# Linear ReLU attention on one core: loads in pairs of octets up to the end, and one order of work for all octets

## The chip, the cores and the metric

The kernel runs on one core of a Trainium2 chip. The metric is the device time of one execution in microseconds (us), as a median of several runs. A profile of one execution stands beside it; its times are counted from the first instruction of the program.

## The reference

Batch 8, 12 heads, sequence 512, head dimension 64, all in fp32. There are 96 heads in all (batch times heads), and each is independent.

```python
Q_feat = np.maximum(0, Q)
K_feat = np.maximum(0, K)
KV = np.einsum('bhkd,bhkv->bhdv', K_feat, V)
K_sum = np.sum(K_feat, axis=2)
numerator = np.einsum('bhqd,bhdv->bhqv', Q_feat, KV)
denominator = np.einsum('bhqd,bhd->bhq', Q_feat, K_sum)
return (numerator / (denominator[:, :, :, None] + 1e-10)).astype(np.float32)
```

Q, K and V are 12 MiB each in HBM, and so is the output.

## The kernel before

The 96 heads are cut into 12 **octets** of eight heads (`NO = 12`). An octet's K, V, Q and output are 1 MiB each in HBM. K and V of an octet come as two **groups** of four heads; octet `o` has the groups `2*o` and `2*o+1`. An octet's rows are spread over the 128 partitions so that each partition reads one contiguous piece.

**Loads.** K, V and Q are cast from fp32 to bf16 on the way, and these DMAs are issued by GpSimd (POOL). Octet 0 is a special case: its K and V are fetched in fp32 by SP and ACT at the start, and its Q by POOL. For octets 1 to 11 there is a ring of `RING = 6` octets in SBUF: `k_all`, `v_all` and `q_all`. Octet `o` lives in slot `(o - 1) % RING`. At the start octets 1 to 6 are fetched as three pairs (`FIRST`), with K, V and Q of a pair as one transfer each. Afterwards `store(o)`, which issues the store of octet `o` on POOL, is followed at once by `load_octet(o + RING)`, which refills the slot of octet `o`. For octets 7 and 8 K, V and Q are one transfer each. From octet 9 on (`PAIRS = NO - 3`) the two groups of K and V are transfers of their own, in the order K, V, K, V, Q. POOL's instructions run in order, so a load that waits holds back the stores and loads after it.

**Compute.** For a group, `prep` makes a masked, rectified copy of K and one masked copy of V on DVE (L195, L197). `prep_v` makes the other copy of V on ACT (L202) or DVE (L204). `kvs(o)` multiplies both groups on PE into `ps_kv` (L209) and evicts the result to `kvd` on ACT (`evac_kv`, L219). `qt(o)` transposes Q on PE (L230) and rectifies it on ACT (L238). `denom(o)` makes the denominators on PE and their reciprocals on DVE (L269 to L281). `out_t(o)` makes the transposed numerators on PE (L260) and copies them to `ot_sb` on ACT (L262). `backs(o)` transposes them back on PE (L287), multiplies them by the reciprocals into an output tile `o_sb` on DVE (L293) and calls `store(o)`. Each engine runs its instructions in the order of the program, which is written by hand (`manual_schedule`). The output tiles come from a pool `outp` of `DELAY + 2 = 7` buffers. The PSUM buffers of `out_t` and of the back transposition are shared: two with the tag `ps_out`.

**Order of a round.** In a steady round `o` the order is: `kvs(o)`, `prep` and `prep_v` of the first group of octet `o+1`, `backs(o-1)`, `denom(o)`, `out_t(o)`, `prep` and `prep_v` of the second group of octet `o+1`, `qt(o+1)`. So an octet's output is finished in the round after its own. From `SAME = NO - 4 = 8` on the order changes: `kvs(o+1)` comes after the second `prep` of the same round, and `backs(o)` stands at the round's end. The last two octets are written out by hand, with the groups of octet 11 multiplied and evicted one at a time, part of the evictions and one rectification on DVE, and the last store in two halves. `idle` issues matmuls whose results are not used.

Of the kernel before, what the change touches and what calls it, by code (L numbers as in the profile page):

```python
# [10 lines left out]
def kernel(  # L11
# [7 lines left out]
    nc = tc.nc  # L19
    B, H, S, D = Q.shape  # L20
    assert D == 64
    P = 128
    D1 = D + 1
# [4 lines left out]
    RQ = S * 8 // P  # L28
    NHG = 4
    U = RQ // 2  # L30
    NG = NH // NHG
    NO = NG // 2
# [3 lines left out]
    fp32 = mybir.dt.float32  # L36
    bf16 = mybir.dt.bfloat16
    Act = mybir.ActivationFunctionType
# [23 lines left out]
    NK = 2  # L62
# [26 lines left out]

    q_sb, k_sb, v_sb = {}, {}, {}  # L90

    PAIRS = NO - 3
    RING = DELAY + 1
    FIRST = (2, 2, 2)
    k_all = consts.tile([P, 2 * RING, R, D], bf16, name="k_all")
    v_all = consts.tile([P, 2 * RING, R, D], bf16, name="v_all")
    q_all = consts.tile([P, RING + 1, U, 2 * D], bf16, name="q_all")
# [6 lines left out]

    def load_kv(X, tile_, first, n):
        to = 2 * ((first // 2 - 1) % RING) + first % 2
        if n == 1:
            nc.gpsimd.dma_start(out=tile_[:, to].rearrange("p r d -> p (r d)"), in_=X[first], single_packet=True)  # L108
            return
        nc.gpsimd.dma_start(out=tile_[:, to:to + n].rearrange("p n r d -> p n (r d)"),  # L110
                            in_=X[first:first + n].rearrange("n p f -> p n f"), single_packet=True)

# [13 lines left out]
    load_q(0)  # L126
    make_identity(nc, ident)

    def load_octet(o, n=1):
        m = 1 if o >= PAIRS else 2 * n  # L130
        for g in range(2 * o, 2 * (o + n), m):
            load_kv(Kr, k_all, g, m)
            load_kv(Vr, v_all, g, m)
        load_q(o, n)

    o = 1
    for n in FIRST:
        load_octet(o, n)
        o += n
    assert o == RING + 1  # L140

    def zero_masks():
        for h in range(NHG):
# [48 lines left out]
    def prep(g):  # L192
        kf[g] = kfp.tile([P, R, 2, D], bf16, name="kf")
        for s in range(2):
            nc.vector.tensor_scalar(kf[g][:, :, s, :], k_sb[g], scalar1=0.0,  # L195
                                    scalar2=mask[:, 0, s:s + 1], op0=Alu.max, op1=Alu.mult)
        nc.vector.tensor_scalar(vo[g % NB][:, :, 0, 2:D + 2], v_sb[g], scalar1=mask[:, 1, 0:1],  # L197
                                scalar2=None, op0=Alu.mult)

    def prep_v(g, eng):  # L200
        if eng is nc.scalar:
            nc.scalar.activation(vo[g % NB][:, :, 1, 2:D + 2], v_sb[g], Act.Copy, scale=mask[:, 1, 1:2])  # L202
        else:
            nc.vector.tensor_scalar(vo[g % NB][:, :, 1, 2:D + 2], v_sb[g], scalar1=mask[:, 1, 1:2],  # L204
                                    scalar2=None, op0=Alu.mult)

    def mm_kv(g):
        for r in range(R):
            nc.tensor.matmul(  # L209
                ps_kv[:, g % 2, 0:2 * (D + 2)].rearrange("p (t d) -> p t d", t=2),  # L210
                kf[g][:, r, :, :].rearrange("p s d -> p (s d)"), vo[g % NB][:, r, :, 1:D4 - 1],
                start=(r == 0), stop=(r == R - 1), skip_group_check=True)


    def evac_kv(o, gs, share=False):
        for s in range(2):
            for c in range(2):
                copy = nc.vector.tensor_copy if share and c == 1 else nc.scalar.copy
                copy(  # L219
                    kvd[o % NK][64 * c:64 * c + 64, 4 * gs.start + s:4 * gs.stop:2,  # L220
                               c * D1:c * D1 + D1].rearrange(
                        "p (g t) d -> p g t d", t=2),
                    ps_kv[64 * s:64 * s + 64, gs, 0:2 * (D + 2)].rearrange(
                        "p g (t d) -> p g t d", t=2)[:, :, :, c:c + D1])


    def transp(o, i):
        ps = pqt.tile([P, U // 2, P], bf16, name="ps_qt")
        for u in range(U // 2):
            nc.tensor.transpose(ps[:, u, :], q_sb[o][:, i * (U // 2) + u, :], ident)  # L230
        return ps

    def relu_q(o, i, ps, eng=None):
        to = qt_sb[o % NZ][:, i * (U // 2):(i + 1) * (U // 2)]
        if eng is nc.vector:
            nc.vector.tensor_scalar(to, ps, scalar1=0.0, scalar2=None, op0=Alu.max)
        else:
            nc.scalar.activation(to, ps, Act.Relu)  # L238

    def qt(o):  # L240
        for i in range(2):
            relu_q(o, i, transp(o, i))


    def idle(n, o):
        for i in range(n):
# [2 lines left out]

    def out_t(o, halves=range(2)):
        if halves[0] == 0:
            ot[o] = otp.tile([P, U, 8, 16], fp32, name="ot_sb")
        q = qt_sb[o % NZ].rearrange("p u (h c) -> p u h c", h=8)
        for j in halves:
            ps = pou.tile([P, 4, U, 16], fp32, name="ps_ot", tag="ps_out")
            for i in range(4):
                h = 4 * j + i
                nc.tensor.matmul(ps[:, i], kvd[o % NK][:, h, 1:2 * D + 1], q[:, :, h, :],  # L260
                                 start=True, stop=True, skip_group_check=True)
            nc.scalar.copy(ot[o][:, :, 4 * j:4 * j + 4], ps.rearrange("p h u c -> p u h c"))  # L262
# [3 lines left out]
    def denom(o):  # L266
        ps = ps_den[:, 0].rearrange("p (u h c) -> p u h c", u=U, h=8)
        for u in range(U):
            nc.tensor.matmul(ps[:, u], qt_sb[o % NZ][:, u, :], kvd[o % NK][:, :, 0:2 * D1:2 * D1 - 1],  # L269
                             start=True, stop=True, skip_group_check=True)  # L270
        own = rcp.tile([P, U, 8, 2], fp32, name="own")
        nc.vector.scalar_tensor_tensor(
            own.rearrange("p u h c -> p u (h c)"), ps.rearrange("p u h c -> p u (h c)"), 1e-10,
            mask_h.rearrange("p h c -> p (h c)").unsqueeze(1).to_broadcast([P, U, 16]),
            op0=Alu.add, op1=Alu.mult)
        den = rcp.tile([P, RQ], fp32, name="den")
        nc.vector.tensor_reduce(out=den.rearrange("p (u c) -> p u c", c=2),  # L277
                                in_=own.rearrange("p u h c -> p u c h"), op=Alu.add,
                                axis=mybir.AxisListType.X)
        rec[o] = rcp.tile([P, RQ], fp32, name="rec")  # L280
        nc.vector.reciprocal(rec[o], den)  # L281
# [9 lines left out]
    def norm(o, j, ps, o_sb):  # L291
        rs = slice(16 * j, 16 * j + 16)
        nc.vector.tensor_tensor(o_sb[:, rs], ps,  # L293
                                rec[o][:, rs].unsqueeze(2).to_broadcast([P, 16, D]), op=Alu.mult)
# [3 lines left out]

    def store(o, o_sb):
        Ov = Or[o].rearrange("p (r d) -> p r d", d=D)  # L300
        if o == NO - 1:
            for j in range(2):
                rs = slice(RQ // 2 * j, RQ // 2 * (j + 1))
                nc.sync.dma_start(out=Ov[:, rs], in_=o_sb[:, rs])
            return
        if o >= NO - 2:
            nc.sync.dma_start(out=Ov, in_=o_sb)
            return
        nc.gpsimd.dma_start(out=Ov, in_=o_sb, single_packet=True)  # L309
        if 0 < o < NO - RING:  # L310
            load_octet(o + RING)

    def out_tile():
        return outp.tile([P, RQ, D], fp32, name="o_sb", tag="o_sb")

    both = slice(0, 2)
    zero8()
    nc.vector.tensor_copy(ident32, ident)
    nc.vector.tensor_reduce(out=mask8k, in_=ident32.rearrange("p (t s b) -> p s t b", t=4, s=2),
# [12 lines left out]
    def backs(o):  # L332
        o_sb = out_tile()
        for j in range(2):
            norm(o, j, back(o, j), o_sb)
        store(o, o_sb)

    def kvs(o):
        mm_kv(2 * o)
        mm_kv(2 * o + 1)  # L340
        evac_kv(o, both)

    SAME = NO - 4
    for o in range(NO - 2):
        if 0 < o <= SAME:
            kvs(o)
        prep(2 * o + 2)
        prep_v(2 * o + 2, nc.scalar)  # L350
        if 0 < o <= SAME:
            backs(o - 1)
        denom(o)
        out_t(o)
        prep(2 * o + 3)
        prep_v(2 * o + 3, nc.vector)
        if o >= SAME:
            kvs(o + 1)
        qt(o + 1)
        if o >= SAME:  # L360
            backs(o)

    o = NO - 2
    g = 2 * NO - 2
    prep(g)
    prep_v(g, nc.vector)
    denom(o)
    out_t(o)
    mm_kv(g)
    evac_kv(o + 1, slice(0, 1))  # L370
    prep(g + 1)
    prep_v(g + 1, nc.vector)

    o_sb = out_tile()
    norm(o, 0, back(o, 0), o_sb)
    ps = back(o, 1)
    mm_kv(g + 1)
    evac_kv(o + 1, slice(1, 2), share=True)
    for i in range(2):
        relu_q(o + 1, i, transp(o + 1, i), nc.vector if i == 1 else None)  # L380
    norm(o, 1, ps, o_sb)
    store(o, o_sb)
    idle(5, o + 1)
    out_t(o + 1, (0,))
    denom(o + 1)
    out_t(o + 1, (1,))
    idle(6, o + 1)
    backs(o + 1)
# [1 line left out]
_INS = ['Q', 'K', 'V']  # L390
_OUTS = [((8, 12, 512, 64), 'float32')]
# [25 lines left out]
```

## Time and profile before

| | |
|---|---|
| time, median of 3 runs | 126.11 us (126.09 to 126.37) |
| profiled execution, its own time | 126.86 us |
| span of that execution, first to last instruction | 125.1 us |
| mean granted TensorE clock | 0.931 |
| busy: PE, DVE, ACT, POOL | 86.3, 83.2, 80.6, 26.5 us |
| read from HBM, written to HBM | 37.75 MB, 12.58 MB |
| DMAs issued on POOL: loads, stores | 31, 10 |
| last store, its two halves issued on SP | 117.78 and 118.91 us |

Busy times are those of the engines themselves; what a sequencer does (waits, DMA issues of SP) is not counted. PE is TensorE, DVE VectorE, ACT ScalarE, SP SyncE. A line number such as L293 is a line of the kernel before. A DMA's landing is the time from its issue until its data is there.

### The profile page before, as it was taken

What the parts mean: (1) busy time and instruction counts of PE and PEld (TensorE: products, weight loads), DVE (VectorE), ACT (ScalarE), POOL (GpSimd) and SP (SyncE); (2) the same over time, 40 slices, a digit from 0 to 9 for tenths busy, and PEclk for the clock granted to TensorE, in tenths of its full rate; (3) what the DMA queues carried; (4) which work ended last, traced back from release to release, by engine and by line L of the source; (5) the groups of instructions that cost most, each with busy time, mean ns of one, the idle gap of its engine ahead of it and who ended that gap; (6) DMA issues with size and microseconds to landing.
All of it is one profiled execution on the core that took longest, in us unless ns stands there. A gap on an engine that the chain in (4) does not pass through costs nothing.

```text
span 125.1 us, 2615 instructions
## 1 busy us (share of the span) xinstructions
PE 86.3 (69%) x1067; PEld 77.6 (62%) x1067; DVE 83.2 (67%) x192; ACT 80.6 (64%) x112; POOL 26.5 (21%) x47
## 2 busy tenths in 40 slices
PE   0005884089898998959989897799596496888500
PEld 0005563089787897839978786698494494876400
DVE  2719716920997979797297984967909819977700
ACT  0009966544989989896598988658669466646000
POOL 6942020000100901203311122144333321000000
PEclk9999999558999999995999999859999999999995
DMA  4999999999999999999999999999999999999991
GB/s 84 389 321 206 212 210 217 214 210 210 215 219 208 212 212 218 214 321 419 217 204 307 282 218 264 324 212 238 347 214 226 356 224 216 349 422 424 430 390 76
DMA packets 9836, 32.67 MB, mean 261 GB/s; under 512 B 736, under 2 KB 736, under 8 KB 8160
## 3 DMA queue, kind: packets, MB, share of 16 engines
q0 software_dynamic: 9104, 28.31, 94.5%
q1 hardware_dynamic: 576, 3.15, 6.6%
q10 hardware_dynamic: 144, 1.05, 2.2%
q8 instruction: 8, 0.13, 0.4%
q14 instruction: 4, 0.03, 0.1%
HBM read 37.75 MB, written 12.58 MB: 402 GB/s over the span
## 4 chain that ended last, share of the span: by engine, by line
DMA 44%; DVE 23%; PE 19%; POOL 4%; ACT 2%; issue 2%; DVEq 1%; POOLq 0%
DMA q_all<-in_Q_dram 28%; DMA v_all<-in_V_dram 16%; DVE o_sb L293 13%; PE ps_kv L209 8%; PE ps_bk L287 6%; PE ps_qt L230 3%; DVE kf L195 3%; ACT ot_sb L262 2%; DVE vo_all L197 2%; PE ps_ot L260 1%; DVE vo_all L204 1%; POOL k_all L110 1%; POOL v_all L110 1%; DVE den L277 1%; DVEq L412 1%
## 5 line engine op out<-in xcount | busy, mean ns | idle before, releaser
L293 DVE TENSOR_TENSOR o_sb<-ps_bk,rec 128x1024 f32<-128x1024 f32 x24 | 28.3, 1218 | 20.0 <-PE ps_bk L287 20.0
L209 PE MATMUL ps_kv<-vo_all,kf 128*128 128x132 bf16 x352 | 26.9, 238 | 4.9 <-DVE vo_all L204 4.4
L209 PEld LDWEIGHTS <-kf 128*128 128x128 bf16 x352 | 24.8, 106 | 6.2 <-issue 3.5
L230 PE MATMUL ps_qt<-ident,q_all 128*128 128x128 bf16 x192 | 15.5, 245 | 15.9 <-DMA q_all<-in_Q_dram 15.8
L262 ACT COPY ot_sb<-ps_ot 128x1024 f32<-128x1024 f32 x24 | 24.0, 1013 | 3.8 <-PE ps_ot L260 2.9
L219 ACT CAST kvd<-ps_kv 64x260 bf16<-64x260 f32 (+1 forms) x46 | 16.5, 359 | 15.1 <-PE ps_kv L209 13.9
L238 ACT ACTIVATE qt<-ps_qt 128x1024 bf16<-128x1024 bf16 x23 | 22.4, 1025 | 3.6 <-PE ps_qt L230 3.5
L230 PEld LDWEIGHTS <-q_all 128*128 128x128 bf16 x192 | 13.7, 111 | 16.9 <-DMA q_all<-in_Q_dram 16.7
L287 PE MATMUL ps_bk<-ident,ot_sb 128*128 128x128 f32 x192 | 23.0, 273 | 0.4 <-ACT ot_sb L262 0.4
L287 PEld LDWEIGHTS ps_bk<-ident,ot_sb 128*128 128x128 f32 x192 | 20.8, 142 | 0.7 <-ACT ot_sb L262 0.7
L195 DVE TENSOR_SCALAR kf<-k_all,mask 128x1024 bf16<-128x1024 bf16 x44 | 18.3, 458 | 1.4 <-DMA k_all<-in_K_dram 1.3
L260 PE MATMUL ps_ot<-qt,kvd 128*128 128x256 bf16 x96 | 13.9, 272 | 6.2 <-DVE o_sb L293 5.5
L260 PEld LDWEIGHTS <-kvd 128*128 128x128 bf16 x96 | 8.9, 97 | 8.8 <-issue 7.0
L309 POOL DMA_DIRECT2D out_dram<-o_sb x10 | 5.5, 551 | 39.8 <-DVE o_sb L293 31.0
L202 ACT ACTIVATE vo_all<-v_all,mask 128x1024 bf16<-128x1024 bf16 x10 | 11.5, 1154 | 1.3 <-DMA v_all<-in_V_dram 1.2
L197 DVE TENSOR_SCALAR vo_all<-v_all,mask 128x1024 bf16<-128x1024 bf16 x22 | 10.6, 483 | 2.1 <-DMA v_all<-in_V_dram 2.1
L269 PEld LDWEIGHTS <-qt 128*128 128x128 bf16 x192 | 6.7, 96 | 4.9 <-ACT qt L238 2.0
L269 PE MATMUL ps_den<-kvd,qt 128*128 128x16 bf16 x192 | 7.3, 179 | 3.0 <-ACT kvd L189 1.7
L178 ACT ACT_TABLE_LOAD x1 | 1.3, 1283 | 9.7 <-DMA v_first<-in_V_dram 9.7
L204 DVE TENSOR_SCALAR vo_all<-v_all,mask 128x1024 bf16<-128x1024 bf16 x12 | 5.8, 480 | 0.0
L110 POOL DMA_DIRECT2D v_all<-in_V_dram x5 | 4.0, 810 | 7.8 <-ACT ot_sb L262 4.4
L108 POOL DMA_DIRECT2D k_all<-in_K_dram x6 | 3.6, 604 | 8.4 <-DMA q_all<-in_Q_dram 4.9
(36 smaller groups left out, 56.7 us busy)
## 6 DMA issues: line engine op xcount, KB each, us to landing
out_dram<-o_sb POOLq DMA_DIRECT2D x10, 1024.0 KB, 15.2
q_all<-in_Q_dram POOLq DMA_DIRECT2D x6, 512.0 KB, 13.8
k_all<-in_K_dram POOLq DMA_DIRECT2D x3, 1024.0 KB, 26.9
v_all<-in_V_dram POOLq DMA_DIRECT2D x3, 1024.0 KB, 31.0
q_all<-in_Q_dram POOLq DMA_DIRECT2D x3, 1024.0 KB, 35.1
k_all<-in_K_dram POOLq DMA_DIRECT2D x6, 256.0 KB, 13.4
v_all<-in_V_dram POOLq DMA_DIRECT2D x6, 256.0 KB, 12.3
v_first<-in_V_dram ACTq DMA_DIRECT2D x1, 1024.0 KB, 8.9
```

The lines of the kernel that those rows point to most:

```text
L195: nc.vector.tensor_scalar(kf[g][:, :, s, :], k_sb[g], scalar1=0.0, scalar2=mask[:, 0, s:s + 1], op0=Alu.max, op1=Alu.mult)
L197: nc.vector.tensor_scalar(vo[g % NB][:, :, 0, 2:D + 2], v_sb[g], scalar1=mask[:, 1, 0:1], scalar2=None, op0=Alu.mult)
L202: nc.scalar.activation(vo[g % NB][:, :, 1, 2:D + 2], v_sb[g], Act.Copy, scale=mask[:, 1, 1:2])
L209: nc.tensor.matmul(ps_kv[:, g % 2, 0:2 * (D + 2)].rearrange("p (t d) -> p t d", t=2), kf[g][:, r, :, :].rearrange("p s d -> p (s d)"), vo[ ...
L219: copy(kvd[o % NK][64 * c:64 * c + 64, 4 * gs.start + s:4 * gs.stop:2, c * D1:c * D1 + D1].rearrange("p (g t) d -> p g t d", t=2), ps_kv[6 ...
L230: nc.tensor.transpose(ps[:, u, :], q_sb[o][:, i * (U // 2) + u, :], ident)
L238: nc.scalar.activation(to, ps, Act.Relu)
L260: nc.tensor.matmul(ps[:, i], kvd[o % NK][:, h, 1:2 * D + 1], q[:, :, h, :], start=True, stop=True, skip_group_check=True)
L262: nc.scalar.copy(ot[o][:, :, 4 * j:4 * j + 4], ps.rearrange("p h u c -> p u h c"))
L269: nc.tensor.matmul(ps[:, u], qt_sb[o % NZ][:, u, :], kvd[o % NK][:, :, 0:2 * D1:2 * D1 - 1], start=True, stop=True, skip_group_check=True)
L287: nc.tensor.transpose(ps[:, 2 * v:2 * v + 2].rearrange("p c d -> p (c d)"), ot[o][:, 8 * j + v].rearrange("p h c -> p (h c)"), ident32)
L293: nc.vector.tensor_tensor(o_sb[:, rs], ps, rec[o][:, rs].unsqueeze(2).to_broadcast([P, 16, D]), op=Alu.mult)
```

## The change

The change has four parts.

- The loads of octets 1 to 10 come as five pairs and octet 11 alone (`RUNS`). K, V and Q of a pair are one transfer each, and so are K, V and Q of octet 11. The first three pairs are issued at the start as before. Octets 7 and 8 are issued after store 1, octets 9 and 10 after store 3, octet 11 after store 4. Before, octets 7 to 11 were issued one at a time after stores 1 to 5.
- All rounds, to the last, have the steady order. The last round has no `prep` or `qt`, and runs `backs(10)` and, at its end, `backs(11)`.
- Both groups of an octet are always evicted together on ACT, and Q is always rectified on ACT.
- The last store is one transfer on SP.

```diff
-    PAIRS = NO - 3
     RING = DELAY + 1
-    FIRST = (2, 2, 2)
+    RUNS = (2, 2, 2, 2, 2, 1)
...
-    def load_octet(o, n=1):
-        m = 1 if o >= PAIRS else 2 * n
-        for g in range(2 * o, 2 * (o + n), m):
-            load_kv(Kr, k_all, g, m)
-            load_kv(Vr, v_all, g, m)
+    def load_octets(o, n):
+        load_kv(Kr, k_all, 2 * o, 2 * n)
+        load_kv(Vr, v_all, 2 * o, 2 * n)
         load_q(o, n)
 
-    o = 1
-    for n in FIRST:
-        load_octet(o, n)
+    o, later = 1, {}
+    for n in RUNS:
+        if o <= RING:
+            load_octets(o, n)
+        else:
+            later[o + n - 2 - RING] = (o, n)
         o += n
-    assert o == RING + 1
+    assert o == NO
...
     def store(o, o_sb):
         Ov = Or[o].rearrange("p (r d) -> p r d", d=D)
-        if o == NO - 1:
-            for j in range(2):
-                rs = slice(RQ // 2 * j, RQ // 2 * (j + 1))
-                nc.sync.dma_start(out=Ov[:, rs], in_=o_sb[:, rs])
-            return
         if o >= NO - 2:
             nc.sync.dma_start(out=Ov, in_=o_sb)
             return
         nc.gpsimd.dma_start(out=Ov, in_=o_sb, single_packet=True)
-        if 0 < o < NO - RING:
-            load_octet(o + RING)
+        if o in later:
+            load_octets(*later[o])
...
-    SAME = NO - 4
-    for o in range(NO - 2):
-        if 0 < o <= SAME:
+    for o in range(NO):
+        if o > 0:
             kvs(o)
-        prep(2 * o + 2)
-        prep_v(2 * o + 2, nc.scalar)
-        if 0 < o <= SAME:
+        if o + 1 < NO:
+            prep(2 * o + 2)
+            prep_v(2 * o + 2, nc.scalar)
+        if o > 0:
             backs(o - 1)
+        if o + 1 == NO:
+            idle(5, o)
         denom(o)
         out_t(o)
-        prep(2 * o + 3)
-        prep_v(2 * o + 3, nc.vector)
-        if o >= SAME:
-            kvs(o + 1)
-        qt(o + 1)
-        if o >= SAME:
-            backs(o)
...
+        if o + 1 < NO:
+            prep(2 * o + 3)
+            prep_v(2 * o + 3, nc.vector)
+            qt(o + 1)
+    idle(6, NO - 1)
+    backs(NO - 1)
```

The part of the program that is left out at the end of the removed lines is the hand-written order of the last two octets. The order of it is: `prep` of group 22 with both copies of V on DVE, `denom(10)`, `out_t(10)`, the product of group 22 and its eviction, `prep` of group 23 likewise, the first half of octet 10's output, the product of group 23 and its eviction shared between ACT and DVE, the transposition of octet 11's Q with one half rectified on DVE, the rest of octet 10's output and its store, then `out_t` and `denom` of octet 11, and `backs(11)`.

More of the change, by code (lines that the diff above doesn't have):

```diff
@@ L106, in load_kv @@
         to = 2 * ((first // 2 - 1) % RING) + first % 2
-        if n == 1:
-            nc.gpsimd.dma_start(out=tile_[:, to].rearrange("p r d -> p (r d)"), in_=X[first], single_packet=True)
-            return
         nc.gpsimd.dma_start(out=tile_[:, to:to + n].rearrange("p n r d -> p n (r d)"),
@@ L212, in mm_kv, with evac_kv @@
                 start=(r == 0), stop=(r == R - 1), skip_group_check=True)
-    def evac_kv(o, gs, share=False):
+    def evac_kv(o):
         for s in range(2):
             for c in range(2):
[L218 to L221, printed above, removed]
+                nc.scalar.copy(
+                    kvd[o % NK][64 * c:64 * c + 64, s::2, c * D1:c * D1 + D1].rearrange(
                         "p (g t) d -> p g t d", t=2),
-                    ps_kv[64 * s:64 * s + 64, gs, 0:2 * (D + 2)].rearrange(
+                    ps_kv[64 * s:64 * s + 64, :, 0:2 * (D + 2)].rearrange(
                         "p g (t d) -> p g t d", t=2)[:, :, :, c:c + D1])
@@ L231, in transp @@
         return ps
[L233 to L238, printed above, removed]
     def qt(o):
         for i in range(2):
-            relu_q(o, i, transp(o, i))
+            nc.scalar.activation(qt_sb[o % NZ][:, i * (U // 2):(i + 1) * (U // 2)], transp(o, i), Act.Relu)
     def idle(n, o):
@@ L248, in idle, with out_t @@
                              skip_group_check=True)
-    def out_t(o, halves=range(2)):
-        if halves[0] == 0:
-            ot[o] = otp.tile([P, U, 8, 16], fp32, name="ot_sb")
+    def out_t(o):
+        ot[o] = otp.tile([P, U, 8, 16], fp32, name="ot_sb")
         q = qt_sb[o % NZ].rearrange("p u (h c) -> p u h c", h=8)
-        for j in halves:
+        for j in range(2):
             ps = pou.tile([P, 4, U, 16], fp32, name="ps_ot", tag="ps_out")
@@ L300, in store @@
         Ov = Or[o].rearrange("p (r d) -> p r d", d=D)
-        if o == NO - 1:
-            for j in range(2):
-                rs = slice(RQ // 2 * j, RQ // 2 * (j + 1))
-                nc.sync.dma_start(out=Ov[:, rs], in_=o_sb[:, rs])
-            return
         if o >= NO - 2:
@@ L309, in store @@
         nc.gpsimd.dma_start(out=Ov, in_=o_sb, single_packet=True)
-        if 0 < o < NO - RING:
-            load_octet(o + RING)
+        if o in later:
+            load_octets(*later[o])
     def out_tile():
         return outp.tile([P, RQ, D], fp32, name="o_sb", tag="o_sb")
-    both = slice(0, 2)
     zero8()
@@ L340, in kvs @@
         mm_kv(2 * o + 1)
-        evac_kv(o, both)
-    SAME = NO - 4
-    for o in range(NO - 2):
-        if 0 < o <= SAME:
+        evac_kv(o)
+    for o in range(NO):
+        if o > 0:
             kvs(o)
-        prep(2 * o + 2)
-        prep_v(2 * o + 2, nc.scalar)
-        if 0 < o <= SAME:
+        if o + 1 < NO:
+            prep(2 * o + 2)
+            prep_v(2 * o + 2, nc.scalar)
+        if o > 0:
             backs(o - 1)
+        if o + 1 == NO:
+            idle(5, o)
         denom(o)
         out_t(o)
-        prep(2 * o + 3)
-        prep_v(2 * o + 3, nc.vector)
-        if o >= SAME:
-            kvs(o + 1)
-        qt(o + 1)
-        if o >= SAME:
-            backs(o)
[L363 to L388, printed above, removed]
+        if o + 1 < NO:
[4 more added lines that the diff above has]
+    backs(NO - 1)
 _INS = ['Q', 'K', 'V']
```

## Prediction

> **What bounds the kernel now.** I read the page first: the DMA row of the slices and the queue table, then stretches of the span.
>
> ```profile
> DMA  4999999999999999999999999999999999999991
> q0 software_dynamic: 9104, 28.31, 94.5%
> q1 hardware_dynamic: 576, 3.15, 6.6%
> ...
> 41.30:51.30 10.00, 9.22 (x136) 8.62 (x137) 8.84 (x21) 9.33 (x12) 3.00 (x5) 1.00 1.12 213
> 61.60:82.20 20.60, 17.29 (x232) 15.79 (x231) 17.28 (x33) 17.91 (x26) 4.34 (x8) 0.96 1.08 260
> 122.00:124.00 2.00, 0.00 (x0) 0.00 (x0) 0.00 (x0) 0.00 (x0) 0.00 (x0) 0.50 0.27 109
> ```
>
> The first three lines are the page's; the others give a stretch, its length, the busy time of PE, PEld, DVE, ACT and POOL, the granted clock, the DMA engines' share and GB/s. The DMA engines are full (0.94 or more in every stretch that I asked for) from 2 us to 122 us. No engine is: PE, DVE and ACT are each busy for about 9 of 10 us at best. So the kernel ends when the data has gone through, as long as the last stores are ready while older stores still wait for the DMA engines. That condition is what I check for the change.
>
> Next, the landings: an issue's start plus "us to landing", asked for one issue at a time. For the transfers issued at 10.97 (V of octets 5 and 6) and 15.90 (Q of 5 and 6):
>
> ```profile
> v_all<-in_V_dram POOLq DMA_DIRECT2D x1, 1024.0 KB, 40.3
> q_all<-in_Q_dram POOLq DMA_DIRECT2D x1, 1024.0 KB, 40.3
> ```
>
> They land at 51.3 and 56.2, and later ones follow in the order of issue. Counted in MiB read from or written to HBM (K, V and Q of one octet are 1 MiB each, a store is 1 MiB): Q of 3 and 4 lands at 41.25, and 6 MiB later, at 56.2, Q of 5 and 6: 2.49 us a MiB in large transfers. From 56.2 to the landing of Q of octet 10 at 99.1 (issue 85.98 plus 13.1) are 17 MiB in smaller transfers: 2.52 us a MiB.
>
> The timeline of POOL's issues shows the issuer:
>
> ```profile
> 51.56 0.70 POOL L110 DMA_DIRECT2D k_all<-in_K_dram  x1 [3.04 <-DMA v_all<-in_V_dram]
> 56.70 0.87 POOL L110 DMA_DIRECT2D v_all<-in_V_dram  x1 [4.45 <-ACT ot_sb L262]
> 61.67 0.55 POOL L309 DMA_DIRECT2D out_dram<-o_sb  x1 [1.83 <-DMA out_dram<-o_sb]
> ```
>
> Each of these starts just after the transfer eight issues earlier has landed (51.3, 56.2, 61.1). So eight are in flight at most, and POOL is blocked for most of the span. That is harmless while eight keep the engines full.
>
> Last, the timeline around the landings at 51.3 and 56.2 (start, duration):
>
> ```profile
> 51.30 0.49 DVE L197 TENSOR_SCALAR vo_all<-v_all,mask 128x1024 bf16<-128x1024 bf16 x1 [0.17 <-DMA v_all<-in_V_dram]
> 52.41 2.35 DVE L293 TENSOR_TENSOR o_sb<-ps_bk,rec 128x1024 f32<-128x1024 f32 x2 [0.62 <-PE ps_bk L287]
> 56.21 1.66 PE L230 MATMUL ps_qt<-ident,q_all 128*128 128x128 bf16 x16 [0.79 <-DMA q_all<-in_Q_dram]
> ...
> 61.68 2.36 DVE L293 TENSOR_TENSOR o_sb<-ps_bk,rec 128x1024 f32<-128x1024 f32 x2 [3.06 <-PE ps_bk L287]
> ...
> 68.78 2.36 DVE L293 TENSOR_TENSOR o_sb<-ps_bk,rec 128x1024 f32<-128x1024 f32 x2 [0.89 <-PE ps_bk L287]
> 72.22 0.78 DVE L195 TENSOR_SCALAR kf<-k_all,mask 128x1024 bf16<-128x1024 bf16 x2
> ```
>
> This stretch is my template. V and Q of an octet pair land late, octet 5 starts at once, and then compute runs unfed for two rounds: one round is 7.10 us (61.68 to 68.78; also 38.22 to 45.31 to 52.41), against 10 us of DMA for an octet (4 MiB). Octet 4's output, held back by the order of the round, starts 5.5 us after Q's landing.
>
> **The change, part by part.**
>
> *Loads in pairs (7 and 8 after store 1, 9 and 10 after store 3, 11 after store 4).* Bytes stay the same; issues on POOL fall from 41 to 29. POOL's issues take 0.53 to 0.87 us each and it idles beside them, so nothing on the path is saved there. The DMA engines save little: 2.52 against 2.49 us a MiB over the 30 MiB after 56.2 is 0.9 us at most, and 0 at least. I take 2.51 for the mixture.
>
> Of the pair, octet 8's load is moved past store 2, octet 10's past store 4, octet 11's past store 5, all on POOL. Those stores come 3 MiB (7.5 us) later, and their readers are the buffers of `outp`: octet 9's output reuses store 2's buffer near 109, and that store lands near 79; hidden. The write-after-read waits (slots of octets 2, 4, 5) ended a round before each issue; nothing new there.
>
> What the pairing does cost is the octet that is wanted first. The queue goes, after 56.2: store 0 (58.8), store 1 (61.1, both already so in this trace), then 2 MiB each of K, V, Q of 7-8, stores 2 and 3, and 2 MiB each of K, V, Q of 9-10. At 2.51: V of 7-8 at 71.2, Q at 76.2; stores to 81.2; K of 9-10 at 86.2, V 91.3, Q 96.3; store 4 at 98.8; octet 11 complete at 106.3. In the trace of before, octet 9's Q lands at 89.2 and octet 10's at 99.1, octet 11's at 109.3. So octet 9 is complete 7.1 us later, 10 and 11 some 3 us earlier, and the early ones are useless until 9 is through.
>
> *The last octets in the steady order.* Removed: halves of the kvd eviction (8 small copies of 0.28 us, two on DVE), octet 11's second relu on DVE (0.69; on ACT 0.97), one masked copy of V, that of group 22, on DVE (0.48; on ACT 1.15). All of these are off the path while PE and DVE wait for each other as in the template. What counts is that an octet's output waits a round: `backs(o)` comes in round o+1, and two `backs` stand in the last.
>
> Now the sum, template shifted by 96.3 - 56.2 = 40.1 us. Octet 8's output starts at 101.8, octet 9's at 108.9. Data for 10 and 11 is there by then, so nothing waits for it. Round 11: kvs at 72.51 + 40.1 = 112.6, its 32 matmuls to 115.1 (2.45 us as in the template's round 7), the first eight transposes of octet 10 (0.9) before its L293 at 115.8, until 118.2. Then PE: five idle matmuls 0.7, denom 0.6, first half of out_t 0.6, ACT's two copies (2 x 1.05) to 120.7, eight transposes 1.1, two L293 2.4: octet 11's output is whole at 124.2. In the trace of before this point is 118.9.
>
> *Last store in one transfer.* Before, the tail of the timeline of SP reads:
>
> ```profile
> 113.65 0.34 SPq L307 DMA_DIRECT2D out_dram<-o_sb  x1
> 117.78 1.46 SPq L304 DMA_DIRECT2D out_dram<-o_sb  x2
> ```
>
> The halves land 5.2 and 5.3 us after their issues, at 123.0 and 124.2, since stores 9 and 10 land only at 121.1 and 121.8: the engines hid the last computation. With the change, octet 9's store is ready at 111.3 and ends near 120, octet 10's at 118.2 and ends near 122; the engines then stand idle until the last store. Bounds for that one: not under 1.0 (issue at 0.74 to first DMA activity at 1.76 at the start) + 2.5 (1 MiB at the 420 GB/s of 110 to 120) + 0.4 = 3.9 us; not over 8.1, which octet 10's took behind others. I take 4.0, near the low end, for nothing is ahead of it. With cover the single transfer would cost at most the 1.1 us between the two issues of before; without it, 512 KB (1.2 us) that could have gone ahead of the second L293. That 1.2 is in the sum.
>
> End: 124.2 + 4.0 = 128.2 landed, + 0.9 from landing to the end (124.2 to 125.1 before) = 129.1 span, 4.0 over 125.1. The profiled execution took 126.86 with 1.76 outside the span, so 130.9 by that clock; it stands 0.75 over the median of 126.11, from which I forecast 126.1 + 4.0 = 130.1 us.
>
> **Rivals.**
>
> *DMA still hides everything (same or a little faster).* The engines were full until 122; if they are again, the end moves only by what 12 fewer issues save, 0 to 0.9 us: 125.2 to 126.1. It needs octet 11's output by 119 to 120, thus Q of 9-10 landed by 92, 2.24 us a MiB over 16 MiB from 56.2. No stretch of the trace is under 2.4. Chance 0.03. The Trainium skill ("DMA: Bandwidth & Descriptors", Rules for kernel authors and Anatomy of one DMA) speaks for this side: it advises 1 MiB or more a transfer and gives each a fixed cost of some 2.0 us, by which 12 fewer would be an estimated 24 us, or about 102 us. The rows go against a cost in series: the five transfers of octet 9 land within 7.4 us of store 3 (81.8 to 89.2) for 3 MiB, 2.47 a MiB, no worse than large ones. Chance of that, 0.01.
>
> *PE stays slow for longer (slower still).* In the template the granted clock falls to 0.68 between 56.2 and 61.6, and kvs takes 3.10 us against 2.2: 1.4 us with qt's 1.66 against 1.06, and this is in my sum. After the change PE also stands still while V of 9-10 is awaited (some 3 us before 93.7), so a second slow stretch may follow: 131.5; with a poor store latency too, 133. Chance 0.1.
>
> *The clock never falls, or the loads run ahead.* Without the 1.4 us and at 2.47 a MiB: 128.2. Chance 0.08.
>
> *Only the single last store matters.* If both halves and order were hidden, at most 1.1 us: 127.2. It needs the same early landing as the first rival. Chance 0.01.
>
> **Numbers.** The forecast has 0.77: its own range 128.8 to 131.6 (2.49 to 2.53 a MiB moves the landing by 0.6, the store by 1). With the neighbours, 128.1 to 132.5. A difference under 0.3%, 0.4 us, couldn't be told from none; between 125.7 and 126.5 falls perhaps half of the first rival: same 0.02, faster 0.03, slower 0.95.
>
> **What would show it.** Right: V and Q of 9-10 land near 91 and 96; L197 waits for V there by some 3 us or more, L230 for Q; octet 8's L293 near 102, then rounds of 7.1 us; the last SP issue near 124; the DMA share drops below 0.5 in the slices around 122 to 125, and the chain ends in a run of DVE, PE and ACT from 96 on. Wrong: the last SP issue before 121, or DMA full until the last microseconds; or a POOL issue in the second half that leaves the engines empty, which would be a wait that I have not counted.

## The result and the profile after

The changed kernel takes 130.97 us (median of 6 runs, 130.30 to 131.78) against 126.17 us before (6 runs in the same session, 126.09 to 126.43). The ratio is 1.0367, with a 95% interval of 1.0339 to 1.0396: slower, by 4.8 us between the medians. Now and then an execution is slower as a whole; ratios are estimated without those, so a ratio need not be the quotient of two medians. The forecast was 130.1. The profiled execution after has a span of 128.6 us and took 130.6 us.

The page's DMA rows of the changed kernel, and then stretches of its span. Columns of a stretch: length, busy time of PE, PEld, DVE, ACT and POOL with counts, granted clock, DMA share, GB/s.

```profile
DMA  3999999999999999999999999999999999993725
q0 software_dynamic: 8912, 28.31, 91.5%
q1 hardware_dynamic: 432, 3.15, 6.1%
...
82.20:102.40 20.20, 15.34 (x180) 13.79 (x179) 12.42 (x25) 13.27 (x19) 1.25 (x3) 0.83 1.10 239
110.00:116.00 6.00, 5.24 (x77) 4.86 (x74) 3.86 (x10) 5.47 (x8) 0.53 (x1) 1.00 1.01 425
116.00:118.00 2.00, 2.00 (x33) 1.90 (x32) 2.00 (x2) 0.72 (x2) 0.00 (x0) 1.00 0.39 160
122.00:124.00 2.00, 0.27 (x3) 0.04 (x1) 1.79 (x2) 0.00 (x0) 0.00 (x0) 1.00 0.00 0
```

The bytes are the same (28.31 MB on POOL's queue). What is new is the end of the DMA row: before, the digits stay at 9 up to the last slice; now four slices read 3, 7, 2 and 5. From 116 us on the DMA engines run dry (share 0.39), and between 122 and 124 they do nothing at all while DVE still works on the last output. Until 116 they are as full as they were.

The landings of V and Q of octets 9 and 10, issued at 59.51 and 61.91:

```profile
v_all<-in_V_dram POOLq DMA_DIRECT2D x1, 1024.0 KB, 31.5
q_all<-in_Q_dram POOLq DMA_DIRECT2D x1, 1024.0 KB, 34.0
```

They land at 91.0 and 95.9. The timeline around it (start, duration, and in brackets the idle time before and what ended it):

```profile
90.99 0.49 DVE L196 TENSOR_SCALAR vo_all<-v_all,mask 128x1024 bf16<-128x1024 bf16 x1 [3.44 <-DMA v_all<-in_V_dram]
91.40 2.35 DVE L281 TENSOR_TENSOR o_sb<-ps_bk,rec 128x1024 f32<-128x1024 f32 x2
95.92 1.89 PE L227 MATMUL ps_qt<-ident,q_all 128*128 128x128 bf16 x16 [1.11 <-DMA q_all<-in_Q_dram]
101.80 2.36 DVE L281 TENSOR_TENSOR o_sb<-ps_bk,rec 128x1024 f32<-128x1024 f32 x2 [4.20 <-PE ps_bk L275]
108.90 2.35 DVE L281 TENSOR_TENSOR o_sb<-ps_bk,rec 128x1024 f32<-128x1024 f32 x2 [0.89 <-PE ps_bk L275]
115.99 2.35 DVE L281 TENSOR_TENSOR o_sb<-ps_bk,rec 128x1024 f32<-128x1024 f32 x2 [2.08 <-PE ps_bk L275]
118.38 5.78 SPq L290 DMA_DIRECT2D out_dram<-o_sb  x2
121.44 2.36 DVE L281 TENSOR_TENSOR o_sb<-ps_bk,rec 128x1024 f32<-128x1024 f32 x2 [1.92 <-PE ps_bk L275]
```

DVE waits 3.44 us for V, PE 1.11 us for Q. From then on nothing waits for a load: octets 8, 9 and 10 come out in rounds of 7.1 us (101.80, 108.90, 115.99), octet 11 at 121.44 to 123.80. SP's row holds two issues; the second takes the last 0.34 us of it, so the last store is issued at 123.82. It lands 3.9 us later.

### The profile page after: what moved, and what is told of

Its sections match the earlier page's. It is cut to its first block, busy times and chain, and to the rows that moved or that the text cites. A ratio compares the mean times of both kernels' runs of the same rounds, so it can differ in the third digit from the quotient of the medians.

```text
span 128.6 us, 2597 instructions
## 1 busy us (share of the span) xinstructions
PE 88.5 (69%) x1067; PEld 79.5 (62%) x1067; DVE 81.8 (64%) x188; ACT 82.7 (64%) x112; POOL 20.9 (16%) x35
## 3 DMA queue, kind: packets, MB, share of 16 engines
q0 software_dynamic: 8912, 28.31, 91.5%
## 4 chain that ended last, share of the span: by engine, by line
DMA 44%; DVE 24%; PE 22%; issue 2%; POOL 2%; DVEq 1%; ACT 1%; ACTq 1%; POOLq 0%
DMA q_all<-in_Q_dram 44%; DVE o_sb L281 12%; PE ps_kv L208 10%; PE ps_bk L275 7%; DVE kf L194 3%; PE ps_qt L227 3%; DVE den L265 2%; DVE vo_all L203 2%; DVE vo_all L196 2%; DVE rec L269 2%; DVE own L260 2%; DVEq L368 1%; ACT ot_sb L250 1%; ACTq L368 1%; POOL v_all L106 1%
## 5 line engine op out<-in xcount | busy, mean ns | idle before, releaser
L281 DVE TENSOR_TENSOR o_sb<-ps_bk,rec 128x1024 f32<-128x1024 f32 x24 | 28.2, 1219 | 23.4 <-PE ps_bk L275 23.4
L208 PE MATMUL ps_kv<-vo_all,kf 128*128 128x132 bf16 x352 | 27.7, 241 | 2.2 <-DVE vo_all L203 2.2
L227 PE MATMUL ps_qt<-ident,q_all 128*128 128x128 bf16 x192 | 16.0, 250 | 18.0 <-DMA q_all<-in_Q_dram 18.0
L208 PEld LDWEIGHTS <-kf 128*128 128x128 bf16 x352 | 25.3, 108 | 3.2 <-issue 3.2
L232 ACT ACTIVATE qt<-ps_qt 128x1024 bf16<-128x1024 bf16 x24 | 23.3, 1025 | 5.7 <-PE ps_qt L227 5.7
L227 PEld LDWEIGHTS <-q_all 128*128 128x128 bf16 x192 | 14.3, 114 | 19.4 <-DMA q_all<-in_Q_dram 19.2
L217 ACT CAST kvd<-ps_kv 64x260 bf16<-64x260 f32 x44 | 16.5, 374 | 10.3 <-PE ps_kv L208 9.4
L248 PE MATMUL ps_ot<-qt,kvd 128*128 128x256 bf16 x96 | 15.4, 288 | 10.6 <-DVE o_sb L281 10.5
L201 ACT ACTIVATE vo_all<-v_all,mask 128x1024 bf16<-128x1024 bf16 x11 | 12.7, 1153 | 4.9 <-DMA v_all<-in_V_dram 4.7
L106 POOL DMA_DIRECT2D v_all<-in_V_dram x6 | 5.1, 843 | 8.8 <-ACT ot_sb L250 4.4
L106 POOL DMA_DIRECT2D k_all<-in_K_dram x6 | 5.0, 828 | 4.1 <-DMA v_all<-in_V_dram 4.1
```

Source lines behind the costliest of these rows:

```text
L208: nc.tensor.matmul(ps_kv[:, g % 2, 0:2 * (D + 2)].rearrange("p (t d) -> p t d", t=2), kf[g][:, r, :, :].rearrange("p s d -> p (s d)"), vo[ ...
L217: nc.scalar.copy(kvd[o % NK][64 * c:64 * c + 64, s::2, c * D1:c * D1 + D1].rearrange("p (g t) d -> p g t d", t=2), ps_kv[64 * s:64 * s + 6 ...
L232: nc.scalar.activation(qt_sb[o % NZ][:, i * (U // 2):(i + 1) * (U // 2)], transp(o, i), Act.Relu)
L281: nc.vector.tensor_tensor(o_sb[:, rs], ps, rec[o][:, rs].unsqueeze(2).to_broadcast([P, 16, D]), op=Alu.mult)
```

## The experiments

Each session ran the kernel before again beside the trials (medians 126.48, 126.47 and 126.28 us); ratios are to those. The rivals are numbered as in the first expectation.

**The loads alone** (kernel before, with the loads of the change):

```diff
-    FIRST = (2, 2, 2)
+    RUNS = (2, 2, 2, 2, 2, 1)
...
-        if 0 < o < NO - RING:
-            load_octet(o + RING)
+        if o in later:
+            load_octets(*later[o])
```

> The order of work, the hand-written end and the two halves of the last store as before; only the loads as after the change. Theory (octets 9 and 10 land as one pair near 91 to 96 us, three octets of work then run with no data to wait for): the order of before takes 9.2 us a round there (L293 at 93.52 and 102.73 in the trace of before), so octet 8's L293 stands near 100.3, octet 9's near 109.5, and the last store issue, 16.2 us later as before, near 125.7: span some 129.3, time 130.8 to 132.0. Rival 1 (the steady order, which holds an output back by a round, is the cause): 126.0 to 126.6. Rival 2 (large transfers are slow in themselves or block POOL): as the theory in the time, but with gaps in the DMA share before 115. Rival 3 (the single last store): 126.0 to 126.6.

131.70 us, ratio 1.0382 (1.0306 to 1.0457). Its DMA row, and the L293 of octets 8 and 9:

```profile
DMA  5999999999999999999999999999999999993545
...
99.97 2.35 DVE L293 TENSOR_TENSOR o_sb<-ps_bk,rec 128x1024 f32<-128x1024 f32 x2 [3.20 <-PE ps_bk L287]
109.15 2.36 DVE L293 TENSOR_TENSOR o_sb<-ps_bk,rec 128x1024 f32<-128x1024 f32 x2 [2.97 <-PE ps_bk L287]
```

The loads by themselves bring the whole loss. The round of the old order is 9.18 us long here, as it was before, and it starts from the same late landing. The DMA row is full up to the last four slices, so POOL left no gap: rivals 1 and 3 are out, and of rival 2 the blocked queue.

**The order alone** (changed kernel, with the loads and the two halves of before):

```diff
-    RUNS = (2, 2, 2, 2, 2, 1)
+    FIRST = (2, 2, 2)
...
-        if o in later:
-            load_octets(*later[o])
+        if 0 < o < NO - RING:
+            load_octet(o + RING)
```

> The steady order to the end, evictions together on ACT; the loads and the two halves of the last store as before. Theory: octet 11's Q lands near 109.3 as before, its kvs starts near 110.4 to 111.1, and 11.2 us later (112.63 to 123.82 in the trace after) the second half is issued at 121.6 to 122.6: span 125.6 to 126.6, time 126.7 to 127.8, so 0.6 to 1.6 us of the 4.8. Rival 1 (order is the cause): 130 to 131. Rivals 2 and 3: 126.0 to 126.6.

127.74 us, ratio 1.0067 (1.0027 to 1.0108): some 0.8 us by the ratio, 1.3 us between the medians. PE waits for Q of octet 11, and the second half is issued at 121.1 (the last 0.34 of the SP row):

```profile
109.44 1.07 PE L228 MATMUL ps_qt<-ident,q_all 128*128 128x128 bf16 x16 [0.51 <-DMA q_all<-in_Q_dram]
120.01 1.46 SPq L293 DMA_DIRECT2D out_dram<-o_sb  x2
```

From Q's landing to the last issue it takes 11.7 us; before, with the two groups of octet 11 handled as they came, 118.9 - 109.25 = 9.7.

**One last store, all else as before:**

```diff
-        if o == NO - 1:
-            for j in range(2):
-                rs = slice(RQ // 2 * j, RQ // 2 * (j + 1))
-                nc.sync.dma_start(out=Ov[:, rs], in_=o_sb[:, rs])
-            return
         if o >= NO - 2:
```

> The kernel before with its last store in one transfer. Theory: stores 9 and 10 land only at 121.1 and 121.8, so the engines are busy when it is issued at 118.9: 0 to 0.4 us more, 126.2 to 126.6. Rival 3 (the single store is a main cause): 128 or more.

126.58 us, ratio 1.0006 (0.9974 to 1.0039): nothing. The engines are still busy when it is issued:

```profile
118.00:120.00 2.00, 0.00 (x0) 0.00 (x0) 0.00 (x0) 0.00 (x0) 0.00 (x0) 1.00 0.97 410
```

**Two halves in the changed kernel** (those lines put into it):

> The changed kernel with its last store in two halves. Theory: at the end the DMA engines stand idle, so the first 512 KB go 1.2 us earlier: 1.2 us less than the changed kernel's 131.0, so 129.4 to 130.2. Rival 3 (the single store is a main cause): 126 to 128. Rival 1 and 2: as the theory, or no difference if the engines are not idle.

130.19 us, ratio 1.0297 (1.0236 to 1.0358). That is 0.8 us under the changed kernel, with intervals that overlap, so the size is not settled by the times. In its trace the second half is issued at 124.59 and the span ends at 128.3, 3.7 us later; with one store it was 4.8 us (123.82 to 128.6). So by the traces the split is worth 1.1 us at this end, and nothing at the end of before: the cover decides.

**Octets 9 and 10 one at a time:**

```diff
-    RUNS = (2, 2, 2, 2, 2, 1)
+    RUNS = (2, 2, 2, 2, 1, 1, 1)
```

> The changed kernel with octets 9 and 10 loaded one at a time, 9 after store 2, 10 after store 3 (RUNS = 2, 2, 2, 2, 1, 1, 1); all else as after the change. Theory: 9's V and Q land near 83.5 and 86, 10's Q near 96, 11's V near 103.4; the rounds from 8 on wait for nothing but some 1 us for 11's V; octet 11's kvs starts near 107.6, the last store is issued near 118.8 and the DMA engines are full until then: span some 124.4, time 125.5 to 126.6, all of the loss gone. Rival 1 (the steady order): 130 to 131. Rival 2 (large transfers): about 129, as the pair 7 and 8 is still there.

126.55 us, ratio 1.0018 (0.9991 to 1.0045): the loss is gone. Octets 8 and 9:

```profile
96.76 2.36 DVE L281 TENSOR_TENSOR o_sb<-ps_bk,rec 128x1024 f32<-128x1024 f32 x2 [0.88 <-PE ps_bk L275]
103.64 0.49 DVE L196 TENSOR_SCALAR vo_all<-v_all,mask 128x1024 bf16<-128x1024 bf16 x1 [1.06 <-DMA v_all<-in_V_dram]
104.04 2.35 DVE L281 TENSOR_TENSOR o_sb<-ps_bk,rec 128x1024 f32<-128x1024 f32 x2
```

Octet 8's output comes 5.0 us earlier than in the changed kernel. The only wait for a load that is left after it is 1.06 us for octet 11's V, as forecast.

**Octets 7 and 8 one at a time, 9 and 10 still a pair** (`RUNS = (2, 2, 2, 1, 1, 2, 1)`):

> The changed kernel with octets 7 and 8 loaded one at a time (7 after store 0, 8 after store 1), and 9 and 10 still as a pair after store 3 (RUNS = 2, 2, 2, 1, 1, 2, 1). Theory: as many MiB as before stand ahead of Q of 9 and 10, so it lands near 96 and the end does not move: 130.3 to 131.7. Rival 2 (large transfers cost in themselves): one pair fewer, about 129.

131.76 us, ratio 1.0403 (1.0348 to 1.0458). Splitting the other pair helps nothing: V and Q of 9 and 10 land at 91.3 and 96.1, as in the changed kernel. The time lies 0.06 above the forecast's range. Two stretches of its span show why it is no faster than the changed kernel:

```profile
88.30:91.70 3.40, 0.00 (x0) 0.00 (x0) 0.43 (x2) 0.37 (x1) 0.00 (x0) 0.50 1.11 217
98.50:101.90 3.40, 3.40 (x31) 3.40 (x30) 0.00 (x0) 0.97 (x2) 0.00 (x0) 0.50 1.12 212
```

Work gets further ahead of the data, PE stands still for longer (0.00 busy), and the granted clock is still 0.50 up to 101.9, so kvs takes 3.73 us instead of 3.29.

**The pair 9 and 10 earlier, first trial.** The load of the pair was placed right behind that of 7 and 8, in round 2.

> The changed kernel with the pair 9 and 10 issued right behind the pair 7 and 8, ahead of stores 2 and 3. The transfers keep their size. POOL then waits for octet 4's slot until about 53, with some 8 us of work still queued. Theory: two MiB fewer go ahead, V lands near 86 and Q near 91, just before octet 8's round wants them (88.1 and 91.7): no wait, the last store issue near 118.8, time 125.5 to 126.6. Rival 2 (large transfers are slow in themselves): 130 to 131. Rival 1 (order): 130 to 131. If the wait for the slot leaves the DMA engines empty, there is a gap near 58 to 62 and the time lies above 127.

168.57 us, and it tells nothing of the question. In the program the load then stands ahead of the reads of octet 3's second group and Q, and of octet 4, in these slots, so those reads wait for octets 9 and 10 and work on their data.

**The pair earlier, second trial:**

```diff
     def store(o, o_sb):
...
+        if o == 2:
+            held.append((Ov, o_sb))
+            return
         nc.gpsimd.dma_start(out=Ov, in_=o_sb, single_packet=True)
+        if o == 1:
+            held.append(later.pop(3))
...
             qt(o + 1)
+        if o == 3:
+            load_octets(*held[0])
+            nc.gpsimd.dma_start(out=held[1][0], in_=held[1][1], single_packet=True)
```

> The changed kernel with the pair 9 and 10 issued at the end of round 3, where octet 4's slot has just been read, and store 2 held back behind it: so stores 2 and 3 come after the pair. The transfers keep their size, the steady order and the single last store stay. Theory: two MiB fewer go ahead, V of 9 and 10 lands near 86 and Q near 91, before octet 8's round wants them (88 and 91.7): the last store issue near 119, time 125.5 to 126.9, as with octets 9 and 10 loaded one at a time. Rival 2 (large transfers are slow in themselves) and rival 1 (the steady order): 130 to 131.

126.42 us, ratio 1.0006 (0.9982 to 1.0030). V is issued at 52.25 and Q at 56.65; their landings, and L281 of octets 6, 7 and 8:

```profile
v_all<-in_V_dram POOLq DMA_DIRECT2D x1, 1024.0 KB, 34.1
q_all<-in_Q_dram POOLq DMA_DIRECT2D x1, 1024.0 KB, 34.6
...
82.87 2.35 DVE L281 TENSOR_TENSOR o_sb<-ps_bk,rec 128x1024 f32<-128x1024 f32 x2 [4.61 <-PE ps_bk L275]
89.96 2.36 DVE L281 TENSOR_TENSOR o_sb<-ps_bk,rec 128x1024 f32<-128x1024 f32 x2 [0.89 <-PE ps_bk L275]
97.06 2.36 DVE L281 TENSOR_TENSOR o_sb<-ps_bk,rec 128x1024 f32<-128x1024 f32 x2 [0.89 <-PE ps_bk L275]
```

They land at 86.4 and 91.3, and the rounds run through at 7.1 us. Here the large transfers, the steady order and the single last store are all in place, and the loss is gone. What cost the time is where the pair lands against the round that wants it. This is the run that decides between the theory and rivals 1 and 2.

**PE kept busy in the wait, first trial** (24 idle matmuls in round 8 of the changed kernel, 16 of them behind `denom`):

> The changed kernel with 24 extra matmuls whose results are not used, in round 8: 16 ahead of out_t, 8 after it, in the time in which PE waits for V and Q of octets 9 and 10. Theory: the granted clock does not fall to half near 93 to 100, so qt takes 1.06 and kvs 2.2 instead of 1.89 and 3.1: 1.5 to 1.7 us less at the end, 129.2 to 129.8. If the clock has nothing to do with PE's idle time there: 130.5 to 131.5, or more by what the extra matmuls delay.

A miss. Its times scatter (130.59 to 133.15), so no ratio is given. The row of the extra matmuls shows what happened:

```profile
94.73 3.51 PE L236 MATMUL ps_den<-q_all,ident 128*128 128x256 bf16 x16 [3.54 <-DVE own L260]
```

They write the tile that DVE's L260 reads, so they waited for it until 94.73 and held up `out_t` behind them.

**Second trial, ahead of `denom`:**

```diff
+        if o == 8:
+            idle(8, o)
+            idle(8, o)
         denom(o)
         out_t(o)
+        if o == 8:
+            idle(8, o)
```

> The changed kernel with 24 extra matmuls whose results are not used in round 8, now 16 of them ahead of denom (in the first trial they stood behind it and waited for DVE to read denom's result) and 8 between out_t and qt. Theory: PE is busy where it waited for V and Q of octets 9 and 10, the granted clock does not fall near 93 to 100, qt takes 1.06 and kvs 2.2 instead of 1.89 and 3.1: octet 8's L281 near 100.2 instead of 101.8, time 129.0 to 129.9 against 131.0. If the clock does not follow PE's idle time there: 130.5 to 131.7.

128.80 us, ratio 1.0188 (1.0150 to 1.0225): 2.2 us less than the changed kernel, and 0.2 below the forecast's range. The stretch from 93.5 to 100.2 in the changed kernel and then in this one, and this one's rows:

```profile
93.50:100.20 6.70, 5.29 (x44) 4.69 (x44) 4.03 (x11) 3.82 (x4) 0.53 (x1) 0.50 1.06 288
93.50:100.20 6.70, 5.67 (x73) 5.28 (x73) 4.44 (x12) 5.04 (x7) 0.53 (x1) 1.00 1.07 290
96.00 1.07 PE L227 MATMUL ps_qt<-ident,q_all 128*128 128x128 bf16 x16 [0.65 <-DMA q_all<-in_Q_dram]
96.90 2.06 PE L208 MATMUL ps_kv<-vo_all,kf 128*128 128x132 bf16 x32
99.88 2.35 DVE L281 TENSOR_TENSOR o_sb<-ps_bk,rec 128x1024 f32<-128x1024 f32 x2 [2.19 <-PE ps_bk L275]
```

Q lands at the same time, the granted clock stays at 1.00, and octet 8's L281 comes 3.88 us after the start of qt instead of 5.88.

**Nothing waits and the store is split:** octets 9 and 10 one at a time, octet 11's load at the end of round 4 and so ahead of store 4, the last store in halves.

```diff
+    RUNS = (2, 2, 2, 2, 1, 1, 1)
...
+        if o == 4:
+            load_octets(*later[4])
```

> Octets 9 and 10 loaded one at a time (9 after store 2, 10 after store 3), octet 11's load issued at the end of round 4, ahead of store 4; the steady order; the last store in two halves. Theory: V of 11 lands near 101, before it is wanted at 102.6, so no round waits; the halves are issued near 117 and 118, with older stores still in the DMA engines until 120 to 121. The end is that of the DMA engines alone: 125.3 to 126.3, against 126.5 with octet 11 after store 4 and a single last store, and 126.2 to 126.5 before the change. If the rest is not DMA, it stays at 126.4 to 127.

126.58 us, ratio 1.0022 (0.9998 to 1.0046), above the forecast's range: no gain. L281 of octet 9 no longer waits for V (104.16, by PE alone), but the engines were already full:

```profile
116.00:118.00 2.00, 1.54 (x15) 1.30 (x12) 1.30 (x2) 0.00 (x0) 0.00 (x0) 1.00 1.01 426
118.00:120.00 2.00, 0.00 (x0) 0.00 (x0) 1.06 (x1) 0.00 (x0) 0.00 (x0) 0.92 0.97 403
```

The span is 124.7 us, the same as with octets 9 and 10 split and octet 11 later. Four versions (before, this one, 9 and 10 split, the pair earlier) end within 0.5% of each other, with the DMA engines at work to about 122. Before and here they are nearly full until then (shares of 0.94 and 0.88 from 120 to 122); in the two with a single last store they have a gap of some 0.6 us between 118 and 120 (shares of 0.73 and 0.68), and it does not show in the time. I found none that beats the kernel before.

## Why the prediction was right

*The landings.* Forecast 91.3 and 96.3 for V and Q of 9 and 10, measured 91.0 and 95.9. The counting of MiB in the order of issue holds; the rate was 2.46 us a MiB (Q of 7 and 8 lands at 76.2, Q of 9 and 10 8 MiB later at 95.9), a little better than the 2.51 taken. Octet 9's store, forecast to end near 120, landed at 118.2; the prediction's own rate would have put it at 96.3 + 9 x 2.51 = 118.9. So the engines ran dry earlier than forecast, which changed nothing, as the next store was ready only at 118.38.

*The template.* Octet 8's L281 was forecast at 101.8 and came at 101.80, rounds of 7.1 us were 7.10 and 7.09, the last issue 124.2 against 123.82. The exact hit of the first is luck, for two errors cancel in it: Q landed 0.4 earlier, and octet 8 took 5.88 us from there, not 5.48, because the clock was at half for nearly the whole of qt and kvs (1.89 and 3.29, against 1.66 and 3.10 in the template).

*The clock term.* 1.4 us was in the sum, though its own rows add up to 1.5 (3.10 - 2.2 and 1.66 - 1.06); keeping PE busy brought 2.0 in the trace and 2.2 in the medians. This term was too small. The rival in which PE stays slow for longer came in part: the clock was at half from 93.4 to 100.3, twice as long as in the template (56.5 to 59.9), but most of the first half lay before Q's landing (95.9), so it cost 0.4 us more and not another 1.4. Whether the clock also explains the scatter of the changed kernel is not shown: of its six runs the shortest span (128.3 us) has the highest mean granted clock, 0.913, and the longest (129.7) the lowest, 0.892, but one of 129.3 has 0.904.

*The last store.* 4.0 us to landing was forecast, 3.9 measured; 1.2 us for the missing split, 1.1 measured in the trace, and nothing where older stores cover it. The prediction's lower bound of 3.9 contains 0.4 us for which it names no row.

*The order.* I let it cost nothing beyond the template's lag. Alone, with the loads of before, it costs some 0.8 us; this does not add to the loads' loss, since with a late pair the old order's rounds of 9.2 us are no better than the steady order's 7.1 (131.70 alone against 130.97 together, intervals overlapping).

*From span to time.* The span grew by 3.5 us and the median by 4.8. I had noted that the profiled execution of before lies 0.75 above its median; the one after lies 0.4 below its own. The sum, made from the span, inherits that: 4.0 was forecast, between the two. For the trace the forecast was 0.5 too long (129.1 against 128.6), by the median 0.9 too short. A sum exact for the trace would have given 126.1 + 3.5 = 129.6, farther from the median; that 130.1 stands nearer is luck, the mechanism is not.

*The rivals.* The DMA engines do hide everything again when Q of the pair lands at 91.3 (126.42 us). That agrees with the condition that I named for that rival, Q by 92, and the changed kernel misses it by 3.9 us. The 0.9 us that fewer issues might save was taken over 30 MiB; 27 follow 56.2 (15 of loads, 12 of stores), which makes it 0.8 and changes nothing. A cost for each transfer in series is out: with octets 9 and 10 split there are 32 issues on POOL, with the pair earlier 29, before 41, and the three times agree to 0.5%. The Trainium skill ("DMA: Bandwidth & Descriptors", Anatomy of one DMA) puts the cost at some 2.0 us a transfer; no run here shows it where the queue is kept full.

## What to carry to other kernels

Merging the loads of two steps into one transfer moves the first step's last byte back by the second step's share; on a full queue, count the bytes ahead of the byte that is wanted first, not the transfers. A DMA-bound kernel stays DMA-bound only while the work that follows the last late landing fits into the transfers still queued: here three unfed rounds of 7.1 us and a tail against 20 us of stores and loads. If merged loads are wanted, issue them ahead of stores that nobody waits for.

## What the runs showed that I had not expected

PE need not stand still for its granted clock to fall. In the kernel before, the clock was 0.50 after a stretch in which PE was busy for 2.08 of 3.41 us; in the changed kernel after 0.79 of 3.41:

```profile
53.09:56.50 3.41, 2.08 (x32) 1.46 (x29) 3.34 (x7) 3.24 (x4) 0.00 (x0) 1.00 1.03 324
56.50:59.91 3.41, 3.41 (x35) 3.41 (x33) 2.12 (x6) 1.94 (x2) 1.41 (x2) 0.50 0.99 396
90.02:93.43 3.41, 0.79 (x12) 0.50 (x9) 2.44 (x3) 1.23 (x2) 0.00 (x0) 1.00 1.07 216
93.43:96.84 3.41, 1.93 (x13) 1.33 (x13) 3.34 (x10) 1.95 (x2) 0.53 (x1) 0.50 1.04 352
```

PE's busy time in such a stretch does not decide it alone either. In the kernel before the clock stayed at 1.00 after a stretch with less of it, 1.76 of 3.42 us:

```profile
87.21:90.63 3.42, 1.76 (x23) 1.45 (x22) 3.27 (x8) 2.26 (x3) 1.31 (x2) 1.00 1.02 344
90.63:94.04 3.41, 3.41 (x47) 3.41 (x47) 0.52 (x1) 2.15 (x5) 1.06 (x2) 1.00 1.12 214
```

With the extra matmuls it stayed at 1.00 after 2.66 of 3.40 us. What decides it stays open. The Trainium skill ("TensorE: Matmul & The Clock Gate", What's actually happening) has the clock fall after an idle window of some 3.4 us. The trace agrees with the two states and with the length (0.50 for 3.4 us before, for twice that after); that the window must be idle it does not bear out.
